# Score products of differential attention in two row halves of TensorE, three passes each, in place of two stacked 128-row passes

## The chip, the cores and the metric

The kernel runs on one core of a Trainium2 chip. The metric is device time in microseconds (us): 1517.39 us before the change, the median of 3 runs (1514.34 to 1518.22).

## The reference

One decoder layer over 2048 tokens of 1024 dimensions, with two branches that read the same normalised input: a state-space layer of 512 channels and causal differential attention of 512 channels. Only the attention's scores are touched:

```
q = q.reshape(bsz, s_len, N_HEADS, 2, HEAD_DIM)      # 4 heads, 2 maps, 64 dimensions
k = k.reshape(bsz, s_len, N_HEADS, 2, HEAD_DIM)
sc = einsum('bhcqd,bhckd->bhcqk', qblk, kt)          # c: the two maps
sc = where(mask, sc, finfo(f32).min)
pr = softmax(sc, axis=-1)
w = pr[:, :, 0] - lam * pr[:, :, 1]
out = einsum('bhqk,bhkd->bhqd', w, vt)               # values of 128 dimensions
```

After it come the output projection of both branches, and a gated per-layer input.

## The kernel before, in words

All large products are made in float32 accuracy from operands of type fp32r that are split in a high and a low part. Two numbers a = ah + al and b = bh + bl give ah·bh + ah·bl + al·bh; the list `passes` (line 702) holds these three pairs.

**Phase 1** (lines 193 to 854) makes the projections, runs the state-space layer in their background, and writes queries and keys to DRAM as high and low parts (`qh_scr`, `ql_scr`, `kh_scr`, `kl_scr`, lines 840 and 841), for each head 128 rows: 64 of the first map, 64 of the second.

**Phase 2** (lines 856 to 1064) is the attention. It goes through 4 heads, and in each through 8 units of 256 queries, in the order `ORD`. A unit loads its queries (`queries`, line 959), and for each of its two blocks of 128 queries goes over the keys in chunks of 512, 384, 256 or 128 columns (lines 990 to 992). For each chunk and each map, TensorE fills a PSUM bank `pss` (line 1005, a ring of `PSS = 3` banks) and VectorE adds the mask, takes the row minimum and writes the scores out (line 1009). Then ScalarE takes the exponentials (line 1018), VectorE or GpSimd joins the two maps (lines 1029 and 1031), TensorE transposes the weights (line 1039), ScalarE copies them (line 1041), and TensorE multiplies them with the values (line 1043). Between the units stand pieces of the state-space half of the output projection (`half`, line 918, products at line 892), which keep TensorE at work where the attention would wait.

How the scores are made before the change: the two halves of TensorE's 128 rows hold one map's parts stacked. `ks[m]` has the map's high keys in rows 0 to 63 and its low keys in rows 64 to 127 (line 954). `qd` has the map's queries in both halves, once the high part (e = 0) and once the low part (e = 1) (lines 959 to 965). One product of 128 rows with e = 0 therefore gives qh·kh + qh·kl, the second with e = 1 gives ql·kh + ql·kl. A map takes two products for each chunk, the two maps four (lines 1004 to 1008).

Nothing but the order of the program and a priority sets the order of the work: the score part of a block is put `SADV = 400` steps ahead (line 988), and the builder of the program then sets a fixed order for every engine. All loads and stores are issued on SyncE's queue, in order.

**Phase 3** (lines 1066 to 1141) is the attention half of the output projection, the gate and the per-layer input.

Of the kernel before, what the change touches and what calls it, by code (L numbers as in the profile page):

```python
# [11 lines left out]
F32 = mybir.dt.float32  # L12
# [7 lines left out]
D = 1024  # L20
# [73 lines left out]
class Streamer:  # L94
    """Runs the making of a sequence of ring tiles ahead of their use."""
# [23 lines left out]
def hymba_kernel(ctx, tc, x_t, p_t, positions, norm_w, w_in, lam_re, lam_im, log_dt, b_re, b_im,  # L119
# [34 lines left out]
    def reduce_angle(pool, src, shape, tag):  # L154
        """src - 2 pi round(src / 2 pi), and its cosine's angle; both within [-pi, pi]."""
        k = pool.tile(shape, F32, name=tag + "k")
        r = pool.tile(shape, F32, name=tag + "r")
        c = pool.tile(shape, F32, name=tag + "c")
        V.tensor_scalar(k, src, 1.0 / TWO_PI, MAGIC, op0=ALU.mult, op1=ALU.add)
        V.tensor_scalar(k, k, MAGIC, None, op0=ALU.subtract)  # L160
        V.scalar_tensor_tensor(r, k, -C1, src, op0=ALU.mult, op1=ALU.add)
        V.scalar_tensor_tensor(r, k, -C2, r, op0=ALU.mult, op1=ALU.add)
        V.scalar_tensor_tensor(r, k, -C3, r, op0=ALU.mult, op1=ALU.add)
        # a quotient next to a half may have been rounded away from its side
        V.tensor_scalar(k, r, 1.0 / TWO_PI, MAGIC, op0=ALU.mult, op1=ALU.add)
        V.tensor_scalar(k, k, MAGIC, None, op0=ALU.subtract)
        V.scalar_tensor_tensor(r, k, -C1, r, op0=ALU.mult, op1=ALU.add)
        V.scalar_tensor_tensor(r, k, -(C2 + C3), r, op0=ALU.mult, op1=ALU.add)
        V.tensor_scalar(r, r, 3.1415925, -3.1415925, op0=ALU.min, op1=ALU.max)
        V.scalar_tensor_tensor(c, r, -1.0, r, op0=ALU.mult, op1=ALU.max)  # L170
        V.tensor_scalar(c, c, -1.0, math.pi / 2, op0=ALU.mult, op1=ALU.add)
        return r, c

    def exp_exact(pool, out_, src, shape, tag):
        """exp to float32's accuracy: 2^k times a polynomial of the rest."""
# [17 lines left out]
    # ------------------------------------------------------------------ phase 1  # L193
    with ExitStack() as p1:
# [3 lines left out]
        # a place for each unit in the ring; what is used last lies lowest  # L198
# [13 lines left out]
        # -- x, split: units of 256 tokens, the model's dimensions on the partitions  # L212
# [32 lines left out]
        def squares(unit):  # L245
            """The mean squares of a unit's tokens, down the partitions."""
# [5 lines left out]
        def norm(hf):  # L252
            """1 / rms of half of the tokens, down the partitions."""
            rs = rstd[:, hf * 8:hf * 8 + 8]
            G.tensor_tensor(rs, rs, negh[:, 0:8], op=ALU.pow)
            # in the order of the tokens, and in that of (l, c)
# [9 lines left out]
        def norm_cols(hf):  # L266
            """The same along the columns of all."""
            rbc[hf] = pc.tile([128, HALF], F32, name="rbc")
            nc.sync.dma_start(rbc[hf], rs_scr[hf].partition_broadcast(128))

        # -- in-projection weights: [128, 512] pairs in the order of use
# [20 lines left out]
        # the first two units and the first weights, in the order of use  # L292
# [15 lines left out]
        # -- state-space layer, in the background of the projections  # L308
        def ssm():
            # tables of rotary embedding and small constants  # L310
            with tc.tile_pool(name="p1s", bufs=1) as sp:
# [16 lines left out]
                # lambda  # L328
# [12 lines left out]
                for nm, src in (("q", q_norm_w), ("k", k_norm_w)):  # L341
                    # the norm's weights: in the rotation's tables, and for what isn't turned down the partitions
# [5 lines left out]
                    if nm == "q":  # L348
                        # scaled by 1 / sqrt(64), and negated: a row's maximum is then minus the minimum, as exp's bias wants it
# [12 lines left out]
                # silu(z) = z (1 + tanh(z / 2)) / 2: the half and 1 - lambda_init go with the weights  # L362
                V.tensor_scalar(subw, subw, float(np.float32(ONE_MINUS)) * 0.5, None, op0=ALU.mult)
                yield
            with tc.tile_pool(name="ssA", bufs=1) as sp:
# [24 lines left out]
                # the parameters of each group that the chunks take from DRAM  # L390
# [36 lines left out]
                # coefficients of the discretisation  # L427
# [17 lines left out]
                # B, discretised: [re; im] and [-im; re] over the partitions  # L445
# [14 lines left out]
                # C: [re; -im] and [-im; -re]  # L460
# [6 lines left out]
                # rotations by the phase of a chunk: its multiples 0..15 and 0..256 by 16  # L467
# [4 lines left out]
                for (Tt, n_) in ((Tb, 16), (Ta, 16)):  # L472
# [3 lines left out]
                    while k < 16:  # L476
                        # e <- f * f, f <- e: the next power of two of the phase
# [11 lines left out]
                # in the tables the sine carries the sign that swaps a state's parts: [+; -]  # L489
                for Tt in (Ta, Tb):  # L490
                    V.tensor_scalar(Tt[1][64:128], Tt[1][64:128], -1.0, None, op0=ALU.mult)
                # decay over a chunk
# [3 lines left out]
                # powers 8..0 of the transition  # L496
# [9 lines left out]
            with tc.tile_pool(name="ssB", bufs=2) as sp:  # L506
                # the norm's factors in the order of (l, c), for each group's rows
                rl = sp.tile([128, NCH], F32, name="rl", bufs=1)
                nc.sync.dma_start(rl, rl_scr.unsqueeze(1).to_broadcast([L, GP, NCH]))
                def split(x_, nm, cols, eng):  # L510
                    """float32 as a pair."""
# [14 lines left out]
                def four(q4):  # L526
                    """For four groups: the parameters, the weights into the state and those within a chunk."""
# [15 lines left out]
                    # D on the diagonal of the last step's rows  # L543
# [8 lines left out]
                    # the block of step l (from the last) starts l steps down  # L552
# [10 lines left out]
                for g in range(NG):  # L563
# [14 lines left out]
                    # table of the rotations: [cos, sin] of chunk 0..256  # L578
# [12 lines left out]
                    # weights out of the state; the steps of a chunk from the last to the first  # L591
# [12 lines left out]
                    def rotate(src, first, op, nm):  # L604
                        """src turned by the phases of the chunks from `first` on, one way or the other."""
# [9 lines left out]
                    # into the state of each chunk, with its phase taken out  # L615
# [19 lines left out]
            with tc.tile_pool(name="ssC", bufs=1) as pg:  # L635
# [13 lines left out]
                for cq in range(8):  # L649
# [7 lines left out]
                    for k in range(4):  # L657
# [3 lines left out]
                        # 2 gelu(y), with the tanh form  # L661
# [8 lines left out]
                    for mp in range(2):  # L670
# [7 lines left out]
                        for e in range(2):  # L678
# [6 lines left out]
                            # (2 sigmoid)(2 gelu)(2 silu) / 8, from (l, c) into the order of the tokens  # L685
# [5 lines left out]
        # -- the projections  # L691
# [13 lines left out]
        for bi, (hf, kind, c0) in enumerate(blocks):  # L705
            leaving = bi == len(blocks) - 1 or blocks[bi + 1][0] != hf
            for t in range(4):
# [5 lines left out]
                if kind in ("u", "zs"):  # L713
                    if kind == "u" and t == 0:
                        ude = [pg1.tile([128, L, 128], F32, name="stg") for _ in range(4)]
                    if bi == 0 and t < 2:
                        # step by step with the arrival of the weights, a bank for each block of columns and unit
# [13 lines left out]
                    elif t in KOUT:  # L731
                        # the weights of two blocks of columns at a time, as they come or go
# [6 lines left out]
                    for cb, k in order:  # L739
# [20 lines left out]
                        elif t in KOUT:  # L760
                            # 2 silu(z)
# [6 lines left out]
                        elif cb % 2 == 1:  # L768
                            # 2 silu(z)
# [86 lines left out]
    # ------------------------------------------------------------------ phase 2  # L856
# [3 lines left out]
    def resident(pool, raws, nm, src, k0, k1, first=0):  # L860
        """Rows of 128 of a weight matrix as split pairs, and what loads them."""
# [11 lines left out]
    def load_y(pool, t, r0, bufs, after=None):  # L873
        """Four blocks of 128 rows of the branches' outputs, split, for 256 tokens."""
# [3 lines left out]
        if after is not None:  # L878
            # not before the attention has come so far
# [6 lines left out]
    def project(pm, w, y, n0):  # L886
        """Two blocks of 128 of the output's dimensions, over half of the branches' outputs."""
# [7 lines left out]
    with ExitStack() as p2:  # L895
# [12 lines left out]
        # 512 columns of nothing, the triangle of a diagonal tile, 128 of all masked  # L908
# [6 lines left out]
        # the state-space half of the output projection, wherever the tensor engine would wait  # L915
# [28 lines left out]
        def head(h):  # L944
            """A head's keys and values, and what loads a quarter of them."""
            pk = (pka, pkb)[h % 2]
            ks = [pk.tile([128, S], F32R, name=f"ks{m}") for m in range(2)]
            vt = pk.tile([128, 16, 128], F32, name="vt")

            def load(c):  # L950
                cs = slice(c * 512, c * 512 + 512)
                for m in range(2):
                    for d, src in enumerate((kh_scr, kl_scr)):
                        nc.sync.dma_start(ks[m][d * 64:d * 64 + 64, cs].bitcast(F32), src[h, m * 64:m * 64 + 64, cs])
# [4 lines left out]
        def queries(h, i):  # L959
            qd = pq.tile([128, 2, 2, 256], F32R, name="qd")  # L960
            for d in range(2):
                for e, src in enumerate((qh_scr, ql_scr)):
                    nc.sync.dma_start(qd[d * 64:d * 64 + 64, e].bitcast(F32),
                                      src[h, :, i * 256:i * 256 + 256].rearrange("(m q) t -> q m t", m=2))
# [4 lines left out]
        for h in range(H):  # L969
# [6 lines left out]
            for i in ORD[h]:  # L976
# [6 lines left out]
                for qt in range(2):  # L983
# [5 lines left out]
                    # columns in pieces of 256 to 512, and those in rows of at most HALF  # L989
# [11 lines left out]
                    for ci, cl in enumerate(chunks):  # L1001
                        end = 640 if ci == len(chunks) - 1 else 512
                        pi, o = where[ci]
                        for m in range(2):
                            pss = ps_s.tile([128, 512], F32, name="pss2")
                            for e in range(2):
                                T.matmul(pss[:, :cl], lhsT=qd[:, e, m, tq], rhs=ks[m][:, c0:c0 + cl],  # L1007
                                         start=e == 0, stop=e == 1)
                            V.tensor_tensor_reduce(  # L1009
                                sr[m][pi][:, o:o + cl], pss[:, :cl], mk[:, end - cl:end], scale=1.0,  # L1010
# [4 lines left out]
                    # row sums of the maps at 12, 13 (and what the second part adds to them at 14, 15)  # L1015
# [8 lines left out]
                    # row sum of the first map times (its softmax - lambda softmax of the second)  # L1024
# [22 lines left out]
                    # mean square and eps, both times the square of the row sum  # L1047
# [18 lines left out]
    # ------------------------------------------------------------------ phase 3  # L1066
    with ExitStack() as p3:
# [11 lines left out]
        def out_proj(i):  # L1079
            """x plus the output projection of 256 tokens."""  # L1080
# [70 lines left out]
def laid_out(inputs):  # L1151
    """The inputs with the axes in the order in which the kernel loads them."""
    a = dict(inputs)
    # [unit of 256 tokens, 128 within, blocks of 128 dimensions, token]
# [34 lines left out]
```

## Time and profile before

| | |
|---|---|
| median of 3 runs | 1517.39 us |
| span of the profiled execution | 1513.9 us |
| TensorE matmul busy | 1423.3 us, 94% |
| VectorE busy | 1015.2 us, 67% |
| ScalarE busy | 755.2 us, 50% |
| GpSimd busy | 648.0 us, 43% |
| DMA traffic | 205.56 MB, 136 GB/s |

The profiled execution shows no time of its own beside its span, the 1513.9 us from its first to its last instruction. It lies 3.5 us under the median of the runs. Engines are called PE (TensorE's products), PEld (its weight loads), DVE (VectorE), ACT (ScalarE), POOL (GpSimd) and SP (SyncE). Products overlap in their records: the record of one product is longer than the distance to the next one, so costs are read from distances between starts.

### The profile page before, as it was taken

What the parts mean: (1) busy time and instruction counts of PE and PEld (TensorE: products, weight loads), DVE (VectorE), ACT (ScalarE), POOL (GpSimd) and SP (SyncE); (2) the same over time, 40 slices, a digit from 0 to 9 for tenths busy, and PEclk for the clock granted to TensorE, in tenths of its full rate; (3) what the DMA queues carried; (4) which work ended last, traced back from release to release, by engine and by line L of the source; (5) the groups of instructions that cost most, each with busy time, mean ns of one, the idle gap of its engine ahead of it and who ended that gap; (6) DMA issues with size and microseconds to landing.
All of it is one profiled execution on the core that took longest, in us unless ns stands there. A gap on an engine that the chain in (4) does not pass through costs nothing.

```text
span 1513.9 us, 27895 instructions
## 1 busy us (share of the span) xinstructions
PE 1423.3 (94%) x9794; PEld 1308.5 (86%) x9794; DVE 1015.2 (67%) x2489; ACT 755.2 (50%) x1711; POOL 648.0 (43%) x902
## 2 busy tenths in 40 slices
PE   7899988997988999999899999899999999999998
PEld 7898887776777888888789888898999999999998
DVE  8579899998999786665377767667779543222222
ACT  8443344544664455533358677677878541111111
POOL 5632666787757341132134445445434442221110
PEclk9999999999999999999999999999999999999999
DMA  7437824334553377634973543544426442111101
GB/s 237 137 114 249 278 82 138 126 88 143 178 155 103 118 187 201 167 119 152 241 213 97 153 137 108 156 122 122 136 80 208 126 152 91 64 63 64 63 22 43
DMA packets 208245, 205.56 MB, mean 136 GB/s; under 512 B 61016, under 2 KB 163560, under 8 KB 207080
## 3 DMA queue, kind: packets, MB, share of 16 engines
q1 hardware_dynamic: 208104, 203.78, 45.0%
q8 instruction: 77, 1.26, 0.3%
q14 instruction: 64, 0.52, 0.1%
HBM read 137.56 MB, written 74.55 MB: 140 GB/s over the span
## 4 chain that ended last, share of the span: by engine, by line
PE 52%; DVE 20%; DMA 12%; POOL 6%; issue 5%; ACT 3%; SPq 2%; DVEq 0%; ACTq 0%; POOLq 0%
PE pm L1125 11%; PE pss L1007 7%; PE pmf L892 7%; PE po L1043 7%; PE pmm L793 6%; PE pm L892 4%; PE ptw L1039 3%; PE pm L1129 3%; DMA wraw<-in_w_in_dram 3%; PE pss L676 2%; PE pmm L747 2%; DVE sw L611 2%; DVE md L612 1%; DVE wl L279 1%; DVE zz L621 1%
## 5 line engine op out<-in xcount | busy, mean ns | idle before, releaser
L793 PE MATMUL pmm<-wl,xh 128*128 128x512 f32 x512 | 202.9, 398 | 2.6 <-DVE wl L279 2.6
L793 PE MATMUL pmm<-wh,xh 128*128 128x512 f32 x512 | 200.2, 397 | 4.5 <-ACT wh L278 4.5
L793 PE MATMUL pmm<-wh,xl 128*128 128x512 f32 x512 | 202.4, 397 | 0.0
L1007 PE MATMUL pss<-ks,qd 128*128 128x512 f32 (+3 forms) x640 | 185.3, 388 | 5.5 <-DMA qd<-qh_scr 3.3
L1018 ACT ACTIVATE s<-s,st 128x1024 f32<-128x1024 f32 (+4 forms) x192 | 171.5, 896 | 35.7 <-DVE st L1009 32.6
L1043 PE MATMUL po<-vt,wt 128*128 128x128 f32 x1088 | 149.6, 276 | 2.3 <-ACT yo L1055 1.3
L1043 PEld LDWEIGHTS po<-vt,wt 128*128 128x128 f32 x1088 | 139.8, 191 | 10.0 <-ACT yo L1055 2.9
L1009 DVE CUSTOM_DVE_ANT_0 s<-pss,mk,st 128x512 f32<-128x512 f32 (+2 forms) x192 | 122.1, 650 | 39.3 <-PE pss L1007 37.9
L1125 PE MATMUL pm<-xh,wgh 128*128 128x256 f32 x512 | 141.3, 282 | 1.9 <-ACT xh L1095 1.8
L1125 PE MATMUL pm<-xh,wgl 128*128 128x256 f32 x512 | 142.8, 281 | 0.0
L1125 PE MATMUL pm<-xl,wgh 128*128 128x256 f32 x512 | 142.4, 281 | 0.0
L747 PE MATMUL pmm<-xh,wh 128*128 128x256 f32 x448 | 125.1, 293 | 8.9 <-DVE stg L757 4.0
L747 PE MATMUL pmm<-xh,wl 128*128 128x256 f32 x448 | 127.7, 289 | 0.7 <-DVE wl L279 0.7
L1133 DVE SCALAR_TENSOR_TENSOR th<-th,pm 128x256 f32<-128x256 f32 x64 | 26.7, 420 | 150.7 <-ACT th L1132 150.7
L747 PE MATMUL pmm<-xl,wh 128*128 128x256 f32 x448 | 127.1, 287 | 0.0
L1096 POOL TENSOR_TENSOR xl<-x,xh 128x512 fp32r<-128x512 f32 x32 | 43.2, 1366 | 179.7 <-PE pm L1125 110.7
L793 PEld LDWEIGHTS pmm<-wh,xh 128*128 128x128 f32 x512 | 97.9, 191 | 23.7 <-ACT wh L278 4.9
L793 PEld LDWEIGHTS pmm<-wl,xh 128*128 128x128 f32 x512 | 97.7, 191 | 23.3 <-DVE wl L279 5.0
L892 PE MATMUL pmf<-yh,woh 128*128 128x256 f32 x352 | 104.2, 296 | 11.5 <-ACT yh L882 9.0
L1007 PEld LDWEIGHTS pss<-ks,qd 128*128 128x128 f32 x640 | 101.3, 192 | 14.7 <-DVE st L1009 4.9
L793 PEld LDWEIGHTS pmm<-wh,xl 128*128 128x128 f32 x512 | 97.9, 191 | 18.3
L1132 ACT ACTIVATE th<-pm 128x256 f32<-128x256 f32 x64 | 24.3, 385 | 166.9 <-PE pm L1129 165.3
(360 smaller groups left out, 4294.5 us busy)
## 6 DMA issues: line engine op xcount, KB each, us to landing
wraw<-in_w_in_dram SPq DMA_DIRECT2D x96, 256.0 KB
xraw<-in_x_t_dram SPq DMA_DIRECT2D x40, 256.0 KB
qd<-qh_scr SPq DMA_DIRECT2D x64, 128.0 KB
qd<-ql_scr SPq DMA_DIRECT2D x64, 128.0 KB
xr<-in_x_t_dram SPq DMA_DIRECT2D x32, 256.0 KB
yin<-yt_scr SPq DMA_DIRECT2D x16, 512.0 KB
xp_scr<-xp SPq DMA_DIRECT2D x32, 256.0 KB
x<-xp_scr SPq DMA_DIRECT2D x8, 1024.0 KB
```

The costliest lines, as they stand in the source:

```text
L611: V.tensor_tensor(sw, sw, tabf[:, 1, first:first + NCH], op=ALU.mult)
L747: T.matmul(pm, lhsT=w[b_][:, cb * 128:cb * 128 + 128], rhs=xt[a_][:, k, :], start=(k == 0 and n == 0), stop=(k == 7 and n == 2))
L793: T.matmul(pm, lhsT=xt[a_][:, k, j * 128:j * 128 + 128], rhs=w[b_], start=(k == 0 and n == 0), stop=(k == 7 and n == 2))
L892: T.matmul(pm[:, e, :], lhsT=w[k][b_][:, ms], rhs=y[a_][:, k, :], start=(k == 0 and n == 0), stop=(k == 3 and n == 2))
L1007: T.matmul(pss[:, :cl], lhsT=qd[:, e, m, tq], rhs=ks[m][:, c0:c0 + cl], start=e == 0, stop=e == 1)
L1009: V.tensor_tensor_reduce(sr[m][pi][:, o:o + cl], pss[:, :cl], mk[:, end - cl:end], scale=1.0, scalar=3.4e38 if ci == 0 else st[:, 2 * ci - ...
L1018: A.activation(sr[m][pi][:, :cl], sr[m][pi][:, :cl], AF.Exp, bias=st[:, ci + m:ci + m + 1], scale=-1.0, accum_out=st[:, 12 + 2 * pi + m:13 ...
L1039: T.transpose(ptw[:, k, :], blocks_[kg + k], ident)
L1043: T.matmul(po[:, 0:128], lhsT=wt[:, k, :], rhs=vt[:, kg + k, :], start=kg + k == 0, stop=kg + k == len(blocks_) - 1)
L1096: G.tensor_tensor(xl, x1[:, n0:n0 + 2], xh.bitcast(F32), op=ALU.subtract)
L1125: T.matmul(pm[:, 0], lhsT=wg[0][k][b_][:, ms], rhs=xc[k // 2][a_][:, k % 2], start=(k == 0 and n == 0), stop=(k == 7 and n == 2))
L1129: T.matmul(pm[:, 1], lhsT=wp[0][k][b_][:, ms], rhs=pc_[a_][:, k], start=(k == 0 and n == 0), stop=(k == 1 and n == 2))
```

## The change

Keys and queries are laid out so that the first map lies in rows 0 to 63 and the second in rows 64 to 127, the high parts in one tile and the low parts in another. For each chunk two PSUM banks are taken at once. Three passes follow (qh·kh, qh·kl, ql·kh), each as two products of 64 rows, one for each map, in the two halves of the rows. Then VectorE empties the two banks one after the other. The product of the two low parts is no longer made.

```
         def head(h):
             pk = (pka, pkb)[h % 2]
-            ks = [pk.tile([128, S], F32R, name=f"ks{m}") for m in range(2)]
+            ks = [pk.tile([128, S], F32R, name=f"ks{e}") for e in range(2)]
             vt = pk.tile([128, 16, 128], F32, name="vt")
 
             def load(c):
                 cs = slice(c * 512, c * 512 + 512)
-                for m in range(2):
-                    for d, src in enumerate((kh_scr, kl_scr)):
-                        nc.sync.dma_start(ks[m][d * 64:d * 64 + 64, cs].bitcast(F32), src[h, m * 64:m * 64 + 64, cs])
+                for e, src in enumerate((kh_scr, kl_scr)):
+                    nc.sync.dma_start(ks[e][:, cs].bitcast(F32), src[h, :, cs])
...
         def queries(h, i):
-            qd = pq.tile([128, 2, 2, 256], F32R, name="qd")
-            for d in range(2):
-                for e, src in enumerate((qh_scr, ql_scr)):
-                    nc.sync.dma_start(qd[d * 64:d * 64 + 64, e].bitcast(F32),
-                                      src[h, :, i * 256:i * 256 + 256].rearrange("(m q) t -> q m t", m=2))
+            qd = pq.tile([128, 2, 256], F32R, name="qd")
+            for e, src in enumerate((qh_scr, ql_scr)):
+                nc.sync.dma_start(qd[:, e].bitcast(F32), src[h, :, i * 256:i * 256 + 256])
             return qd
...
+                        pss = [ps_s.tile([128, 512], F32, name="pss2") for _ in range(2)]
+                        for n_, (a_, b_) in enumerate(passes):
+                            for m in range(2):
+                                r_ = slice(m * 64, m * 64 + 64)
+                                T.matmul(pss[m][:, :cl], lhsT=qd[r_, a_, tq], rhs=ks[b_][r_, c0:c0 + cl],
+                                         start=n_ == 0, stop=n_ == 2)
                         for m in range(2):
-                            pss = ps_s.tile([128, 512], F32, name="pss2")
-                            for e in range(2):
-                                T.matmul(pss[:, :cl], lhsT=qd[:, e, m, tq], rhs=ks[m][:, c0:c0 + cl],
-                                         start=e == 0, stop=e == 1)
                             V.tensor_tensor_reduce(
-                                sr[m][pi][:, o:o + cl], pss[:, :cl], mk[:, end - cl:end], scale=1.0,
+                                sr[m][pi][:, o:o + cl], pss[m][:, :cl], mk[:, end - cl:end], scale=1.0,
```

## Rows read from the trace of the kernel before

**Rows 1.** The page: the span, and the busy time of each engine.

```profile
span 1513.9 us, 27895 instructions
PE 1423.3 (94%) x9794; PEld 1308.5 (86%) x9794; DVE 1015.2 (67%) x2489; ACT 755.2 (50%) x1711; POOL 648.0 (43%) x902
```

**Rows 2.** Stretches of the span, attention in the first: busy us of each engine.

```profile
core 0: us, PE busy (x) PEld busy (x) DVE busy (x) ACT busy (x) POOL busy (x), PEclk, DMA share, GB/s
...
740.00:1190.00 450.00, 428.74 (x3160) 398.80 (x3160) 331.86 (x942) 323.18 (x776) 200.77 (x365) 0.98 0.50 141
1190.00:1514.00 324.00, 315.18 (x2640) 313.18 (x2639) 94.53 (x180) 70.79 (x147) 73.11 (x66) 1.00 0.22 75
```

**Rows 3.** Line 1007 by itself: count, ns min/median/max, starts, chunks by width.

```profile
L1007 PEld LDWEIGHTS pss<-ks,qd x640: 186/190/333, 751.7 to 1185.8; 128*128 128x128 f32 x160
L1007 PE MATMUL pss<-ks,qd x640: 221/393/774, 751.9 to 1186.0; 128*128 128x512 f32 x100, 128*128 128x256 f32 x28, 128*128 128x384 f32 x28, 128*128 128x128 f32 x4
```

**Rows 4.** Timeline of PE, 762 to 803: start us, us, line, shape, count.

```profile
762.11 0.28 PE L892 MATMUL pmf<-yh,woh 128*128 128x256 f32 x1
762.23 0.29 PE L892 MATMUL pmf<-yh,wol 128*128 128x256 f32 x1
...
764.38 1.08 PE L1007 MATMUL pss<-ks,qd 128*128 128x512 f32 x4
765.30 0.49 PE L1039 MATMUL ptw<-ident,s 128*128 128x128 f32 x3
...
768.13 0.51 PE L1007 MATMUL pss<-ks,qd 128*128 128x384 f32 x2
768.49 0.60 PE L1043 MATMUL po<-vt,wt 128*128 128x128 f32 x4
768.85 0.71 PE L1007 MATMUL pss<-ks,qd 128*128 128x512 f32 x2
769.40 0.38 PE L1043 MATMUL po<-vt,wt 128*128 128x128 f32 x2
...
802.07 1.05 PE L1043 MATMUL po<-vt,wt 128*128 128x128 f32 x8
802.96 0.60 PE L1039 MATMUL ptw<-ident,s 128*128 128x128 f32 x4
```

**Rows 5.** Timeline near 900 us: a weight load beside the product before it.

```profile
899.88 0.28 PE L892 MATMUL pmf<-yh,woh 128*128 128x256 f32 x1
899.88 0.19 PEld L892 LDWEIGHTS pmf<-yh,wol 128*128 128x128 f32 x1
...
900.00 0.28 PE L892 MATMUL pmf<-yh,wol 128*128 128x256 f32 x1
```

**Rows 6.** Timeline of DVE near 902 us: two banks emptied.

```profile
901.66 0.74 DVE L1009 CUSTOM_DVE_ANT_0 s<-pss,mk,st 128x512 f32<-128x512 f32 x1
...
902.33 0.08 DVE L1009 DVE_READ_ACCUMULATOR2_ANT st<- 128x1 f32 x1
```

**Rows 7.** Waits of PE and PEld at line 1007: us, times, longest us.

```profile
PE pss L1007 <- DMA qd<-qh_scr: 3.3, 2, 1.6
PE pss L1007 <- DVE st L1009: 1.5, 1, 1.5
...
PE pss L1007 <- DMA qd<-ql_scr: 0.6, 1, 0.6
PEld pss L1007 <- DVE st L1009: 4.9, 12, 1.7
PEld pss L1007 <- DMA qd<-ql_scr: 1.0, 2, 0.8
```

**Rows 8.** Loads of queries and keys, SyncE's queue: issue ns min/median/max.

```profile
L963 SPq DMA_DIRECT2D qd<-qh_scr x64: 573/597/1254, 708.5 to 1172.8; - x64
L963 SPq DMA_DIRECT2D qd<-ql_scr x64: 573/604/1558, 709.8 to 1173.5; - x64
...
L954 SPq DMA_DIRECT2D ks<-kh_scr x32: 445/546/1298, 720.4 to 985.0; - x32
L954 SPq DMA_DIRECT2D ks<-kl_scr x32: 444/588/603, 720.9 to 985.6; - x32
```

## The prediction

> **What bounds the kernel now.** The page comes first: TensorE's products are busy for 1423.3 of 1513.9 us, the next engine for 1015.2 [rows 1]. An average over phases says little, so the stretches come next: in the attention, from 740 to 1190 us, PE works 428.7 of 450 us, DVE 331.9 (74%) and ACT 323.2 (72%), and after it PE works 315.2 of 324 [rows 2]. PE is the bound in both, with 21 us of idle time in the attention. A time that PE no longer needs there can come off the end, as long as DVE and ACT stay behind it; a time that PE needs more comes on at once. Last I read line 1007 alone: 640 products and 640 weight loads, for 100 chunks of 512 columns, 28 of 384, 28 of 256 and 4 of 128, which is 160 chunks with four products each [rows 3].
>
> The records (median 393 ns) overlap, so I take distances between starts [rows 4]. Four products of 512 columns start at 764.38 and what follows at 765.30: 0.23 us each. Two of 384 go from 768.13 to 768.49: 0.18. Products of 256 stand 0.12 apart (762.11 and 762.23). Eight of 128 columns go from 802.07 to 802.96: 0.111 each; these stream a quarter of the 512's columns in half its time, so I read 0.111 us as the pace of the weight loads, one for each product. Scores now cost 400 × 0.23 + 112 × 0.18 + 112 × 0.12 + 16 × 0.111 = 92.0 + 20.2 + 13.4 + 1.8 = **127.4 us** of PE.
>
> **The products.** Four products a chunk become six, each of 64 rows, two for each pass, in different halves of the rows. Whether two products in the two halves stream side by side, no row shows: every product here has 128 rows. Bounds: side by side with their weight loads, a pass costs one distance, three for four: 127.4 × 3/4 = 95.6, a gain of 31.8 us. Not side by side at all: six for four, 191.1, a loss of 63.7. Between them lies a case in which the products run side by side but the loads go in turn: 960 loads at 0.111 make 106.6 us alone. A pass then takes the larger of 0.23 and 2 × 0.111 = 0.222: 100 × 3 × 0.23 + 60 × 3 × 0.222 = 69.0 + 40.0 = 109.0, a gain of 18.4; and if the second half trails the first by one load at the end of each chunk, 160 × 0.111 = 17.8 of that is lost, leaving 0.6. This case has a point that a mean hides: chunks of 256 columns go from 4 × 0.12 = 0.48 to 0.67 us and get slower, those of 384 from 0.72 to 0.67, only those of 512 from 0.92 to 0.69. The rows show that a load already runs beside another product's stream (the load at 899.88 starts with the product before its own) [rows 5], which speaks for much overlap, so I take the mean of 31.8, 18.4 and 0.6: **17 us gained**.
>
> The Trainium skill, "TensorE: Matmul & The Clock Gate", section "Measured speedup vs the span model", gives 3.07 times the speed for four products packed by rows. As an estimate from that page, 3.07/4 is 77%, so two halves would give 1.53, and 191.1/1.53 = 125 us, a gain of 2; no run here shows it, and my sum does not use it.
>
> **The switches.** Scores alternate with products of 128 rows (transposes, values, projection). If each chunk is one run of six, there are 160 runs and 320 changes between 64 and 128 rows. What such a change costs, no row shows. The nearest is a change of line and width at 128 rows: between 768.13 and 769.40 three runs take 0.36 + 0.36 + 0.55 us, against 0.36 + 0.44 + 0.46 by their distances, so nothing on balance [rows 4]. The other end is that the stream must empty at each change. A record outlasts the distance by 1.08 − 0.92 = 0.16 us, and with a weight load that could not go ahead it is 0.27: 320 × 0.16 = 51 us, or 320 × 0.27 = 86. Below nothing is possible by a little, since six in a row replace mostly pairs. I take 0.025 us, near the nearer row, as **8 us lost**.
>
> **PSUM and VectorE.** The ring keeps three banks; a chunk now takes two at once, and both are finished only at its third pass. VectorE empties a bank in 0.67 us (from 901.66 to 902.33) and reads its minimum in 0.08 [rows 6], so a chunk needs 1.5 us there, as before. But the next chunk's second product waits until the first bank is free, and PE works in order: what is queued behind that product waits too, transposes and values, then ACT's copies. PE and PEld wait 1.5 + 4.9 us for this now [rows 7]. The cover is the other work in PE's order: of 428.7 us some 300 is not scores, 1.9 us a chunk, more than the 1.5. I add half of today's wait, **3 us lost**; bounds nothing, and 160 × 0.67 = 107 if no other work stood between, which that cover excludes; I carry 15 as the upper end.
>
> **Loads.** Queries go from 128 issues to 64 and half the bytes, keys from 64 issues to 32 with the same bytes [rows 8]. An issue takes 0.6 us of SyncE's queue, so a unit's queries arrive 1.2 us sooner. PE waits for them 3.3 + 0.6 + 1.0 = 4.9 us in five waits [rows 7]. At 1.2 us a wait nearly all could go; some of it is one wait seen by both queues. I take **3 us gained**; bounds nothing and 8, since the start of the attention also stands behind these issues. The work of DVE, ACT and POOL keeps its instructions and sizes; leaving out the product of the low parts costs nothing anywhere. If scores come sooner, what is late next is DVE: with 332 us of work in what would be some 440 it is at 75%, not yet a bound.
>
> **Sum.** −17 + 8 + 3 − 3 = −9 us. The profiled span is 3.5 us under the median of the runs; I take that difference as unchanged, so the forecast is 1517.4 − 9 = **1508 us**. Its own range: all ends good, −31.8 − 8 gives 1478; with no gain but the smallest it meets the next case.
>
> **The rivals.**
>
> *The loads eat it.* Products side by side, weight loads in turn with the trailing half: −0.6, DVE +3, loads −3, switches nothing: 1517 us, no change. For it speaks that 86% of the span is already weight loads [rows 1] and that products of 128 columns go at the pace of loads [rows 4]; against it, that a load in one half need not hold the other's.
>
> *The array empties at each change of rows.* Place: PE, before and after each chunk's six. Price 51 us at 0.16: −17 + 51 + 3 − 3 = +34, 1551 us; with the better product case (−31.8) 1537, with 0.27 a change 1586. It decides from 17/320 = 0.053 us a change, where the gain is used up. For it: a full-height product cannot share the array with a half-height stream still draining, and the runs are short. Against it: no change of shape in the rows costs anything. The Trainium skill, "TensorEngine Tiling (Array Packing)", section "Key Properties", says that changing the tiling mode drains TensorE; no row here shows whether it does.
>
> *It does not do what it says.* The two halves stream one after the other: +63.7 + 3 − 3, or 1581 us, more with switches. For it, only that no row shows an overlap of two streams; against it, that their rows and banks are disjoint.
>
> **How the numbers follow.** The forecast has 0.42, the loads' case 0.20, the emptying array 0.26, no overlap 0.12. A measurement of this kernel can tell about 0.3%, or 4.6 us, from no change. The forecast is faster, the loads' case the same, the other two slower: 0.42, 0.20 and 0.38. Cases of both signs hold most of the chance: the likeliest one's own range is 1485 to 1513. The range for all must leave out no more than 2 in 10: without the last case (0.12) and the upper part of the third (about 0.06) it ends at 1560, and it begins at 1488, since all the best ends together are unlikely.
>
> **What would show it.** Right: at line 1007, 960 products; the two of a pass start within a few hundredths of a us of each other; a run of six at 512 columns takes about 0.7 us to the next line's start, against 0.92 for four; the attention's stretch is some 9 us shorter. Chunks of 256 tell whether loads go in turn: 0.36 us for a run if not, 0.67 if so. A gap of 0.05 us or more on either side of every run would show the third case, 1.4 us for a run of six at 512 the fourth. Waits of PE for line 1009 well over 10 us would show that the pair of banks was mis-sized, and DVE over 85% in the stretch that PE is no longer the bound. The prediction is wrong above all if the distance of a pair, or the price of a change of rows, is not what I took from rows of 128.

## The result, and the profile after

The changed kernel takes 1634.38 us (median of 4 runs, 1631.14 to 1639.44) against 1515.87 us for the kernel before on the same chip: 1.0781 times the time, with an interval of 1.0752 to 1.081. It is 118 us slower, where 9 us faster was forecast, and its time lies above the range.

The head of the page of the changed kernel, to be held against [rows 1]:

```profile
span 1637.7 us, 28385 instructions
## 1 busy us (share of the span) xinstructions
PE 1562.6 (95%) x10114; PEld 1349.2 (82%) x10114; DVE 1019.8 (62%) x2489; ACT 760.6 (46%) x1711; POOL 646.6 (39%) x902
```

DVE, ACT and POOL do the same work as before to within 6 us. PE is busy for 139 us more, and the weight loads for only 41, though there are 320 more of them. Where it went is seen in the stretches (columns as in [rows 2]):

```profile
740.00:1190.00 450.00, 444.88 (x2701) 339.37 (x2699) 259.06 (x739) 252.21 (x600) 157.57 (x287) 0.99 0.33 96
1190.00:1314.00 124.00, 124.00 (x802) 98.21 (x801) 76.65 (x209) 77.96 (x183) 43.78 (x82) 1.00 0.30 94
1314.00:1638.00 324.00, 315.75 (x2642) 313.55 (x2640) 94.76 (x173) 68.74 (x140) 73.48 (x62) 1.00 0.22 73
```

The last stretch is the 324 us of before, and the attention's 450 us have become 574. PE is busy in 569 of these at nearly the full clock (0.99 and 1.00 granted), so neither a wait of PE nor the clock takes the 124 us. But PE does its 3503 products at a slower pace, and the weight loads idle: they are busy for 437.6 us of 574, where before they were for 398.8 of 450.

What the products look like is in the timeline of PE (columns as in [rows 4]):

```profile
901.75 0.97 PE L1007 MATMUL pss<-ks,qd 64*128 64x512 f32 x6
902.65 1.16 PE L1044 MATMUL po<-vt,wt 128*128 128x128 f32 x8
903.64 0.71 PE L1040 MATMUL ptw<-ident,s 128*128 128x128 f32 x5
904.28 0.96 PE L1007 MATMUL pss<-ks,qd 64*128 64x512 f32 x3
905.17 0.39 PE L892 MATMUL pmf<-yh,woh 128*128 128x256 f32 x1
...
909.22 0.55 PE L1007 MATMUL pss<-ks,qd 64*128 64x128 f32 x3
909.70 0.55 PE L1040 MATMUL ptw<-ident,s 128*128 128x128 f32 x3
...
911.63 0.63 PE L1007 MATMUL pss<-ks,qd 64*128 64x256 f32 x6
912.19 1.38 PE L1044 MATMUL po<-vt,wt 128*128 128x128 f32 x10
```

A run is here a row of products of line 1007 with no other line's product between them. Six products of 512 columns take 0.90 us (901.75 to 902.65), and three take 0.89 (904.28 to 905.17). So six cost no more than three: the halves do stream side by side. But three streams of 0.23 are 0.69, not 0.89, and three of 128 columns take 0.48 (909.22 to 909.70) instead of 0.33: each run carries 0.15 to 0.2 us beyond its streams. And most runs are runs of three. The order of PE in the built program has 274 runs at line 1007: 233 of three, each in one half alone, 32 of six, nine others. In the trace, too, a run of three at 512 columns never takes less than 0.88 us, three streams and the 0.2. The kernel before has 266 runs, mostly of two. The six products of a chunk, written map after map within each pass, did not stay together. The reading is that the ring has three banks, so the second bank of a chunk is still with VectorE when the first is free, and the builder's order puts the three products of the free bank first and the other three later, with other lines between. What speaks for it comes below: in the four runs that take both banks as one tile, every run is of six products or a multiple of six.

The waits of the weight loads show the rest (us, times, longest; "issue" is idle time that no semaphore explains):

```profile
PEld po L1044 <- issue: 23.0, 68, 0.5
PEld pmf L892 <- issue: 17.7, 53, 0.4
PEld ptw L1040 <- issue: 12.8, 37, 0.4
PEld pss L1007 <- issue: 7.5, 44, 0.3
...
PEld pss L1007 <- DVE st L1010: 4.5, 10, 3.0
```

All but those of line 1007 stand in front of lines of 128 rows. In the kernel before, issue takes under 1 us in the whole span but for one time:

```profile
PEld pss L1007 <- issue: 1.8, 1, 1.8
```

Waits for VectorE are as small as they were [rows 7], and those for the queries are gone.

### The profile page after: what moved, and what is told of

It reads as the page before. It is cut to its first block, busy times and chain, and to the rows that moved or that the text cites. A ratio compares the mean times of both kernels' runs of the same rounds, so it can differ in the third digit from the quotient of the medians.

```text
span 1637.7 us, 28385 instructions
## 1 busy us (share of the span) xinstructions
PE 1562.6 (95%) x10114; PEld 1349.2 (82%) x10114; DVE 1019.8 (62%) x2489; ACT 760.6 (46%) x1711; POOL 646.6 (39%) x902
## 4 chain that ended last, share of the span: by engine, by line
PE 62%; DVE 16%; DMA 10%; issue 4%; POOL 4%; ACT 3%; SPq 2%; DVEq 0%; ACTq 0%; POOLq 0%
PE pss L1007 13%; PE pm L1126 10%; PE po L1044 9%; PE pmf L892 8%; PE pmm L793 7%; PE ptw L1040 4%; PE pm L892 4%; PE pm L1130 3%; DMA wraw<-in_w_in_dram 2%; PE pss L676 2%; PE pmm L747 1%; DVE md L612 1%; DVE wl L279 1%; DVE sw L611 1%; DVE xl L220 1%
## 5 line engine op out<-in xcount | busy, mean ns | idle before, releaser
L1007 PE MATMUL pss<-ks,qd 64*128 64x512 f32 (+3 forms) x960 | 242.6, 393 | 2.8 <-DVE st L1010 2.8
L1007 PEld LDWEIGHTS pss<-ks,qd 64*128 64x128 f32 x960 | 132.6, 185 | 48.8 <-issue 7.5
L1044 PE MATMUL po<-vt,wt 128*128 128x128 f32 x1088 | 163.9, 287 | 1.3 <-ACT yo L1056 1.3
L1010 DVE CUSTOM_DVE_ANT_0 s<-pss,mk 128x512 f32<-128x512 f32 (+3 forms) x128 | 78.9, 630 | 84.5 <-PE pss L1007 77.1
L1042 ACT COPY wt<-ptw 128x512 f32<-128x512 f32 (+3 forms) x160 | 80.0, 519 | 74.1 <-PE ptw L1040 58.9
```

The lines of the kernel that those rows point to most:

```text
L1007: T.matmul(pss[m][:, :cl], lhsT=qd[r_, a_, tq], rhs=ks[b_][r_, c0:c0 + cl], start=n_ == 0, stop=n_ == 2)
L1010: V.tensor_tensor_reduce(sr[m][pi][:, o:o + cl], pss[m][:, :cl], mk[:, end - cl:end], scale=1.0, scalar=3.4e38 if ci == 0 else st[:, 2 * c ...
L1042: A.copy(wt[:, :nk], ptw[:, :nk])
L1044: T.matmul(po[:, 0:128], lhsT=wt[:, k, :], rhs=vt[:, kg + k, :], start=kg + k == 0, stop=kg + k == len(blocks_) - 1)
```

## The experiments

The theory after the result, **A**: two halves overlap wherever both stand in one run, most runs hold one half only, and every run of 64-row products costs some 0.4 us at its two ends. **B**: products of 64 rows are slow by themselves and overlap is the exception. **C**: the loss is PE's waiting for the second bank. **D**, added later: keeping the pairs together is all that was missing.

### Taking the two losses apart

**Six products, no change of rows.** The kernel before, with a third product for each chunk and map (the one of the low queries, made twice, so the scores differ a little):

```
-                            for e in range(2):
-                                T.matmul(pss[:, :cl], lhsT=qd[:, e, m, tq], rhs=ks[m][:, c0:c0 + cl],
-                                         start=e == 0, stop=e == 1)
+                            for n_, e in enumerate((0, 1, 1)):
+                                T.matmul(pss[:, :cl], lhsT=qd[:, e, m, tq], rhs=ks[m][:, c0:c0 + cl],
+                                         start=n_ == 0, stop=n_ == 2)
```

> The kernel before with a third product of 128 rows for each chunk and map (the one of the low queries made twice, so the scores differ a little): six products a chunk one after the other, in some 274 runs as in the changed kernel, with no change of rows. Theory A: only the streams, 63.7 us over before, 1570 to 1590 us. Theory B: the same 63.7 us, and the changed kernel's other 60 us stay unexplained by it unless 64-row products are slower than 128-row ones. Theory C: some 1640 us, as the changed kernel, since the waits for the banks are alike.

Measured: 1565.6 us, 1.035 times before (1.0303 to 1.0398), or 54 us more, in 274 runs as in the changed kernel. Theory A's range was 4 us too high, and C's 1640 fell. B expected the same as A here.

**The change of rows, no additional products.** The changed kernel with two of its three passes (the product of the low queries and the high keys is left out):

```
-                        for n_, (a_, b_) in enumerate(passes):
+                        for n_, (a_, b_) in enumerate(passes[:2]):
...
-                                         start=n_ == 0, stop=n_ == 2)
+                                         start=n_ == 0, stop=n_ == 1)
```

> The changed kernel without its third pass (the product of low queries and high keys is left out): four products of 64 rows a chunk, as many as before has of 128, in some 250 runs. Theory A: 250 runs at 0.4 us are 100, less before's own 20, less a little overlap: 1580 to 1600 us. Theory B with slow 64-row products: 640/960 of the changed kernel's score time, so about 1560 us. Theory C and a loss from the number of products alone: 1510 to 1525 us, as before.

Measured: 1577.35 us, 1.0428 times before (1.0387 to 1.0469), or 66 us more, with the same number of products as before and 251 runs. It falls 3 us short of A's range and 17 over B's 1560, and C and "the number of products alone" fall by over 50 us. The two together make 54 + 66 = 120 us, the 118 of the change. The losses add up, so there are two of them.

### Streams alone

**Products by themselves**, with no semaphores between them and the layer left out: 96 of each kind, then 16 rounds of each mixture. Two of the kinds, the halves in turn and three and three, at 512 columns:

```
+    for k in range(6 * R):
+        h = (h0, h1)[k % 2]
+        T.matmul(bk[k % 2][:, :512], lhsT=xr[h, w(k)], rhs=xr[h, 1024:1536], start=True, stop=True)
...
+    for k in range(6 * R):
+        h = (h0, h1)[k // 3 % 2]
+        T.matmul(bk[k // 3 % 2][:, :512], lhsT=xr[h, w(k)], rhs=xr[h, 1024:1536], start=True, stop=True)
```

> Streams of products alone, the layer left out: 96 of full rows, of one half, of the halves in turn, of three and three, at 512 and 256 columns, then repeated changes between 64 and 128 rows. Theory A: 0.23 us for each product of full rows and of one half alone at 512; 0.115 for the halves in turn and for three and three alike; at 256 columns 0.06 in turn if the loads of the two halves overlap, 0.111 if they go in turn; three products of one half at 512 and six of full rows at 256 take 0.69 + 0.72 + 0.4 = 1.8 us a round, the same with six of both halves, and 1.41 with full rows throughout. Theory B: 0.23 for the halves in turn too, and 1.4 and 2.1 us for the two mixed rounds. Theory D: 1.41 us for both mixed rounds.

The timeline of PE: line 119 is full rows at 512 columns, 122 one half, 126 the halves in turn, 130 three and three, 134 in turn at 256, 137 one half at 256, 140 full rows at 256; then the rounds with one half (144, 146), both halves (151, 153) and full rows (157, 159).

```profile
36.98 21.92 PE L119 MATMUL bk<-xr 128*128 128x512 f32 x96
58.83 21.62 PE L122 MATMUL bk<-xr 64*128 64x512 f32 x94
80.08 0.50 PE L126 MATMUL bk<-xr 64*128 64x512 f32 x1
80.30 0.39 PE L122 MATMUL bk<-xr 64*128 64x512 f32 x1
80.42 0.39 PE L126 MATMUL bk<-xr 64*128 64x512 f32 x1
80.52 0.39 PE L122 MATMUL bk<-xr 64*128 64x512 f32 x1
80.65 11.14 PE L126 MATMUL bk<-xr 64*128 64x512 f32 x94
91.41 11.28 PE L130 MATMUL bk<-xr 64*128 64x512 f32 x96
102.51 5.93 PE L134 MATMUL bk<-xr 64*128 64x256 f32 x96
108.26 11.68 PE L137 MATMUL bk<-xr 64*128 64x256 f32 x96
119.87 11.77 PE L140 MATMUL bk<-xr 128*128 128x256 f32 x96
131.56 0.96 PE L144 MATMUL bk<-xr 64*128 64x512 f32 x3
132.45 0.98 PE L146 MATMUL bk<-xr 128*128 128x256 f32 x6
133.36 0.96 PE L144 MATMUL bk<-xr 64*128 64x512 f32 x3
...
162.16 0.96 PE L151 MATMUL bk<-xr 64*128 64x512 f32 x6
163.06 0.98 PE L153 MATMUL bk<-xr 128*128 128x256 f32 x6
163.96 0.96 PE L151 MATMUL bk<-xr 64*128 64x512 f32 x6
...
190.48 0.86 PE L157 MATMUL bk<-xr 128*128 128x512 f32 x3
191.18 0.87 PE L159 MATMUL bk<-xr 128*128 128x256 f32 x6
191.89 0.86 PE L157 MATMUL bk<-xr 128*128 128x512 f32 x3
```

Distances from one line's start to the next, divided by the count, give the prices; the granted clock is 1.00 from 36 to 211 us. Full rows at 512: 21.85/96 = 0.228 us. Of one half, the last of 96 starts at 80.52, so (80.52 − 58.83)/95 = 0.228 each: a half is as long as a whole. Halves in turn: from 80.65 to 91.41, 10.76/94 = 0.114 each, and three and three 11.10/96 = 0.116. At 256 columns in turn: 5.75/96 = 0.060, against 11.61/96 = 0.121 for one half. So two halves stream fully side by side, in both orders, and their weight loads overlap too: each of these products has its own load, and 0.060 is about half of the 0.111 that was read as the pace of the loads [rows 4].

The rounds give the change of rows: 133.36 − 131.56 = 1.80 us with three products of one half, 163.96 − 162.16 = 1.80 with six of both, and 191.89 − 190.48 = 1.41 with full rows. 0.39 us a round, for two changes: **0.195 us a change**, the same with three 64-row products between as with six. About 0.21 of it lies behind the 64-row products (132.45 − 131.56 = 0.89, less 3 × 0.228) and 0.18 in front of them (133.36 − 132.45 = 0.91, less 6 × 0.122). The idle time of the weight loads that was seen in the layer is there as well, in front of the full rows, once in each mixed round, and in no round of full rows alone:

```profile
PEld bk L146 <- issue: 5.8, 16, 0.4
PEld bk L153 <- issue: 5.8, 16, 0.4
```

Theory A's numbers hold, and B and D fall here.

### Keeping the pairs together in the layer

Does the change gain where its six products stay in one run? That needs two pairs of banks, and all eight banks are taken. So each try but the last takes a bank from somewhere, and each has the kernel before with the same banks as its control. The edit for the pairs is the same in all:

```
-                        pss = [ps_s.tile([128, 512], F32, name="pss2") for _ in range(2)]
+                        pss2 = ps_s.tile([128, 2, 512], F32, name="pss2")
+                        pss = [pss2[:, m] for m in range(2)]
```

**The fourth bank from the projection's pieces**, which share the transposes' ring:

```
-                    pm = ps_f.tile([128, 2, 256], F32, name="pmf")
+                    pm = ps_w.tile([128, 4, 128], F32, name="ptw").rearrange("q a b -> q (a b)").rearrange("q (e t) -> q e t", e=2)
```

> Pairs kept, with four banks for scores and two for outputs; the fourth bank is the one of the projection's pieces, which share the transposes' ring instead. 130 runs of score products. Theory A, with the prices of the streams measured alone (a pair costs one stream, 0.39 us a run for its two changes of rows): 95.6 + 130 x 0.39 = 146 us of score time, against 127.4 + 208 x 0.09 = 146 for its control: within 15 us of the control, on either side. Theory B (no overlap in the layer): some 95 us over the control. Theory D (changes of rows cost nothing here): 40 to 50 us under the control.

> Control of the run with shared banks: the kernel before with four banks for scores and the projection's pieces in the transposes' ring. All theories: 1520 to 1600 us, by what the shared ring costs.

Measured: 1577.86 us with pairs (1.0402 times before, 1.0372 to 1.0433), 1577.01 us for the control (1.0407, 1.0387 to 1.0426). They are equal, as A has it; B's 95 us over the control and D's 40 to 50 under it fall. The groups at the scores' line, first with pairs, then the control (busy, mean ns, idle before and what ended it):

```profile
L1008 PE MATMUL pss<-ks,qd 64*128 64x512 f32 (+3 forms) x960 | 137.5, 399 | 15.3 <-DVE st L1011 15.1
```

```profile
L1007 PE MATMUL pss<-ks,qd 128*128 128x512 f32 (+3 forms) x640 | 177.1, 388 | 12.1 <-DMA qd<-qh_scr 5.7 <-DVE st L1009 4.4 <-DMA qd<-ql_scr 1.8
```

PE is busy at the scores for 40 us less, with half as many products again. By the distances between starts, summed over the timeline from 745 to 1240 us with the idle times left out, the scores go from 149.7 us in the control to 129.7 with pairs; the other lines of PE, unchanged in number, go from 292.4 to 315.4. The gain of 20 us, which already bears the change behind each run, is paid back at the entries: 130 runs × 0.18 to 0.195 = 23 to 25. The granted clock is nearly the same in both, 0.97 with pairs and 0.96 in the control (740 to 1245 us).

**The fourth bank from the outputs**, whose ring goes from two banks to one:

> The changed kernel with the two banks of a chunk as one tile of two banks, two such tiles (the outputs' ring gives up one bank), so that the six products of a chunk become ready together and stand in one run: 129 runs of score products instead of 274. Theory A (products in the two halves overlap whenever both halves stand in one run, and each run of 64-row products costs about 0.4 us of emptying and refilling at its two ends): streams 95.6 us plus 129 x 0.4 = 52, about 148 us, as much as before's 127 plus some 20 of its own run starts, so 1505 to 1540 us, near the kernel before. Theory B (64-row products are slow by themselves, each of the 960 at some 0.2 us or more, and overlap is the exception): near the changed kernel, 1600 to 1640 us. Theory C (the loss is PE waiting for the second bank): well under before's time, 1480 to 1505, since the waits go and the overlap stays.

> The kernel before with the same banks as the run with pairs kept: four single banks for scores, one for outputs. A control: theories A and B expect 1500 to 1530 us, within 1% of before; if it is slower, that much of the run with pairs kept is the outputs' bank.

Measured: 1653.0 us (1.0928, 1.0899 to 1.0956) and 1670.02 us (1.1035, 1.0999 to 1.1071). Both expectations missed: these banks cost the control 158 us, where I had expected less than 1%. PE now waits for the outputs' chain, 38.1 us with pairs and 39.1 in the control at the outputs' transpose alone. With pairs it is 17 us under its control, but with some 80 and 95 us of idle PE in the attention the two can't be compared as products.

**The same, with the outputs copied out of their bank early**:

```
+                    A.copy(pc_o, po[:, 0:128])
...
-                    T.transpose(po[:, 128:256], ya, ident)
+                    T.transpose(pto[:, 0, :], ya, ident)
```

> The pairs kept in one tile of two banks, two such tiles, and the outputs' bank freed early by a copy, so that one bank for outputs does not hold up the attention: 139 runs of score products. Theory A (overlap within a run, about 0.4 us for each run of 64-row products): 95.6 + 139 x 0.4 = 151 us of score time against 127 + 192 x 0.08 = 143 for its control, so 0 to 20 us over the control. Theory B (64-row products do not overlap): 191 + 56 = 247, so some 100 us over the control. Theory D (keeping the pairs is all that was missing, the change of rows costs nothing): 95.6 against 143, so 30 to 45 us under the control.

> The control of the run with copied outputs: the kernel before with the same banks and the same copy. All theories: 1510 to 1560 us; 64 copies and their waits are all that is new against before.

Measured: 1779.96 and 1778.97 us (1.1748, 1.172 to 1.1776, and 1.1736, 1.17 to 1.1777). Equal, but the control missed its 1510 to 1560 by over 200 us. The transposed output now takes a bank of the transposes' ring, and PE waits at this transpose for VectorE's `ya`, its input: 132.3 us with pairs and 149.7 in the control. Why that wait grew was not taken apart. Where PE waits so much, this says nothing of the products.

**One pair and no third bank**, against the kernel before with two banks:

> The changed kernel with the pair as one tile of two banks and no third bank, all else as in the changed kernel: 143 runs. Theory A: 95.6 + 143 x 0.4 = 153 us of score time against the changed kernel's 164 of streams and 274 x 0.4 = 110, so up to 120 us under the changed kernel by the products; the two banks alone cost waits for VectorE of 0.2 to 0.5 us a chunk, so 1540 to 1610 us. Theory B: 1640 us or more.

> Control of the run with pairs in two banks (1672 us): the kernel before with two banks for scores. If two banks alone cost what the idle time there shows (some 90 us of PE), 1570 to 1640 us; theory A wants the pairs within 20 us or more of it, since with 143 runs their score time is 139 us by the trace, against 127 and the run starts of the stacked products; theory B wants them some 100 us over it.

Measured: 1671.76 us (1.1032, 1.0994 to 1.1071), against 1545.53 us (1.0203, 1.0176 to 1.0229). Theory A missed with both: it gave 1540 to 1610 us for the pair and wanted the two within some 20 us, and they are 126 apart, more like the 100 of B. The control came in under its 1570 to 1640. But the products are not what differs: six at 512 columns take 0.90 us here too, and the distances at the scores' line sum to 143 us, against 160 in the control. The waits of PE at the scores, with one pair and then with two single banks:

```profile
PE pss L1008 <- DVE st L1011: 47.9, 48, 2.8
```

```profile
PE pss L1007 <- DVE st L1009: 11.1, 30, 1.2
```

Single banks go back one at a time, so PE fills one while VectorE empties the other. A pair goes back whole: PE waits for both, and then VectorE waits for PE. The stretch of the attention shows the rest, again first with the pair (columns as in [rows 2]):

```profile
740.00:1355.00 615.00, 518.70 (x3687) 423.28 (x3686) 338.34 (x947) 331.13 (x780) 201.55 (x366) 0.92 0.29 87
740.00:1235.00 495.00, 461.95 (x3275) 412.91 (x3275) 337.63 (x954) 330.30 (x794) 204.58 (x379) 0.98 0.44 130
```

PE is idle for 96 us with the pair and for 33 in the control, 63 us more. And the granted clock is 0.92 against 0.98: TensorE is at the lower of its two levels, 1.2 of 2.4 GHz, for a larger part of a stretch in which PE idles more. As an estimate from these lines, 615 × 0.08 less 495 × 0.02 makes some 40 us more of lost clock. Idle time and clock thus account for up to some 100 of the 126 us, and here theory C is at work after all. What share each has, beside the changes of rows of the 143 runs, was not measured by itself.

## Why the prediction was wrong

**What bounds the kernel** held: PE is the bound before and after, and DVE and ACT stayed behind it.

**The products** were priced right for what was meant and wrong for what was built. The best bound was the true one: a pair costs one stream, the loads overlap, and the step's mean of 31.8, 18.4 and 0.6 was too low for six products in one run. But the step that failed first is the sentence "If each chunk is one run of six, there are 160 runs". I took the order of the loops for the order of PE. The kernel's order comes from the builder, by what is ready; the step on PSUM even says that the second product waits for a bank, and prices it as 3 us of idle time. That wait did not become idle time (waits for line 1010 are 7.3 us where they were 6.4); it became an order in which the halves are apart. With that, most passes cost what the fourth case said, six streams for four: 54 us in the run without a change of rows, where 17 us of gain had been forecast.

**The switches** were the second failure, by size: 0.025 us a change, taken near a row in which nothing about the rows changes, where 0.195 was measured. The rival's price of 0.16 from a record's tail was near (that the tail is what a change waits for is not shown), and its deciding point, 0.053, was far exceeded. With 274 runs the two changes of each cost 274 × 0.39 = 107 us; the kernel before lost some 0.07 a run at its own starts (by distances its scores take 145.7 us, against 127.4 for the streams), 18 us in 266 runs, so some 89 are new, where 8 were forecast. The run with two passes gave 66 of such a loss, with 251 runs, 49 of which held both halves and gained by their overlap. By the Trainium skill's rule that a change of tiling mode drains TensorE ("TensorEngine Tiling (Array Packing)", section "Key Properties"), such a loss was to be expected, and the trace agrees: 0.39 us in each round of two changes.

In the changed kernel itself 39 runs hold both halves, so its streams cost less than the 54 of the run with full rows. By distances its scores take 223.5 us; less 274 × 0.21 behind the runs, 166 are streams, 39 more than 127.4. As an estimate, then, 39 us of streams and 89 of changes make 128, near the attention's 124.

**The rivals** were set up as alternatives, each with its own time. Two of them held at once. Their prices, 51 us of emptying and 64 of streams one after the other, would have made 115, near the 118 that came, but by luck: the emptying was under-priced, and part of the streams did overlap (89 and 39 by the estimate above). The range ended at 1560 because the fourth case was cut off as unlikely and no case held both.

**The loads** held: with half as many issues for the queries, no wait for them is left at line 1007, where there were 4.9 us [rows 7]. **PSUM** failed in kind, as told. What would show it was well chosen: a run of six at 512 columns and the gap beside each run show the cause in the first profile.

With the order mended and the banks equal, the change is worth nothing: 20 us gained at the scores' line, 23 lost at the others. No version run here beats the kernel before. By the prices, a version with longer runs of 64-row products might: as an estimate, two chunks in a run cost 2 × 0.69 + 0.39 = 1.77 us, against four pairs at 0.46, or 1.84, and the starts of before. But it needs banks that this layer doesn't have, and was not run.

## What to carry to other kernels

Products in two halves of the rows ran at twice the pace here, in both orders that were tried, where they stood in one run on PE. Price a run at its streams plus about 0.4 us, and count the runs in the built order, not in the loops. Where half-height products are mixed finely with full-height ones, stacking the parts to full height can be cheaper than halving the streams, as it was here. And a change that takes PSUM in larger pieces can change the order of the work before it shows as a wait: here the products of one chunk moved apart.

## What was not expected of the hardware

Products in different halves pass each other. In the streams alone, products of line 126 start at 80.08 and 80.42 us, ahead of products of line 122 at 80.30 and 80.52 that stand before them in the program. And three and three (0.116 us each) go nearly as fast as in turn (0.114). If products started in their order and only halves overlapped, six products in threes would take four streams, as an estimate 4 × 0.228/6 = 0.152 us each. The Trainium skill, "TensorE: Matmul & The Clock Gate", section "The mechanism", has products strictly in order in start and end; here the records and the pace of three and three differ, across the halves, and the measurement decides. And two halves gave 0.228/0.114 = 2.0 times the pace, where the prediction's estimate from the Trainium skill's figure for four (same page, section "Measured speedup vs the span model") was 1.53.
